# Hybrid decoder block: when the last gate/up products ask for the down projection's operands

## The chip, the cores and the metric

The kernel runs on one core of one Trainium2 chip. The metric is device microseconds (us) of one execution, lower is better. The kernel before took 987.95 us, the median of three runs (984.64, 988.54 and 987.95). Its profile is of a further execution, which took 985.37 us.

## The reference, cut to what matters

A sequence of 1024 tokens (after 16 meta tokens) of width 1024 goes through one decoder block in float32: a normalised mixer with two convolution groups, a residual, and then a SwiGLU feed-forward of width 2816 whose output is normalised, scaled by a gain and added to the residual. The change touches the feed-forward alone:

```python
def swiglu(xn, w_gate, w_up, w_down):
    a = jnp.einsum("btd,df->btf", xn, w_gate)
    u = jnp.einsum("btd,df->btf", xn, w_up)
    return jnp.einsum("btf,fd->btd", jax.nn.silu(a) * u, w_down)

        ff = swiglu(rms_norm(h, pre_ffn_norm[l]), w_gate[l], w_up[l], w_down[l])
        h = h + rms_norm(ff, post_ffn_norm[l])
```

## The kernel before, in words

**Arithmetic.** Each float32 operand is split into a rounded part (hi, written by ScalarE as a cast) and a rest (lo, written by VectorE as a difference), and one product of 128 by 128 by 512 is three matmuls: hi·hi, hi·lo, lo·hi (`mm3`, lines 106 to 110). The order of work on each engine is written out by hand: instructions stand on an engine in the order in which the Python code emits them, and each waits by semaphore for what it reads and for the buffer that it overwrites. A buffer belongs to a pool and a tag with a fixed number of copies, taken in turn.

**Gate and up.** The 2816 columns are 22 tiles of 128 (f tiles), taken as `NP` = 11 pairs; pair `j` holds f tiles `j` and `j + 11`. For each pair, gate and up are computed for two halves of the tokens and two halves of the 1024 inner columns by seven block products instead of eight. They are named 1, 6, 2, 5, 7, 3, 4 and run in this order from the third pair on; each is 24 matmuls, twelve for gate and twelve for up. After each product its sums leave PSUM (`Pair.leave`). With product 4 of a pair the SwiGLU outputs are complete, and `Pair.sums` forms the four sums S1 to S4 that the down projection needs of them, on GpSimd. `Pair.split` later turns each of the pair's seven results (A11, A12, A22, S1 to S4) into hi and lo and writes them to DRAM (`gdA`, `gdS`), hi through the buffer `HI`, which has four places.

**Down.** The down projection is seven block products too, in the order 1, 5, 2, 6, 7, 3, 4, each over 11 steps, one for each pair `j`. A step is 12 matmuls on four token tiles of 128. It reads `a`, 512 KB loaded back from DRAM by GpSimd's queue (`load`), and `db`, hi and lo of a sum of `w_down` tiles `wb`, which ScalarE and VectorE make two steps ahead (`side`, `LEAD` = 2). `a` goes into the tags `ws` and `wh` by turns, three copies each; `db` goes into the tag `wl`, three copies. In product 4, the last, the six last `j` of each token tile are kept for the end and run token tile by token tile, so that the epilogue of one tile runs beside the next; the `a` of `j` = 9 and 10 are put into `wl` there.

**Around the change from one to the other.** In the loop over pairs and products, `s` counts the products. With the last pair, `load_b` asks for `w_down`: 256 KB pieces on SyncE's queue for the first block of columns (`wb00`, `wb01`, `wb02`), 1 MB transfers on ScalarE's queue for later blocks (`wb10`, `wb11`). `gB_out` is the output gain, 512 KB, spread over 128 partitions. In `run`, at step `s` = 1, `last()` takes product 4 of the last pair out of PSUM, the ScalarE table is changed, and `gB_out` is multiplied by a constant on ScalarE (line 1124). The built program gives the transfers of SyncE and ScalarE eight completion semaphores in turn; the issue of one waits until the transfer that had its semaphore before has landed.

The lines that the steps below touch: 108 to 110 (matmuls), 644, 647, 650 (the add, subtract and multiply helpers), 767 and 769 (`glu`), 777 to 780 (`split`), 970 (`load_b`), 983 (`load`), 1024 and 1124 (`gB_out`), 1052 (output), 1099 and 1100 (`side`).

Of the kernel before, what the change touches and what calls it, by code (L numbers as in the profile page):

```python
# [9 lines left out]
F32R = mybir.dt.float32r  # L10
# [45 lines left out]
def hybrid_block(ctx: ExitStack, tc: tile.TileContext, xT, x, w_in, w_out, w_gate, w_up, w_down, par, g_post, g_ffn, g_out, out):  # L56
# [586 lines left out]
    def add(o, a, b, eng=None):  # L643
        (eng or nc.vector).tensor_tensor(o, a, b, op=ALU.add)  # L644
# [4 lines left out]
    def mul(o, a, b, eng=None):  # L649
        (eng or nc.vector).tensor_tensor(o, a, b, op=ALU.mult)  # L650
# [21 lines left out]
    class Pair:  # L672
# [62 lines left out]
        def leave(self, n, m, p):  # L735
            v, j = self.v, self.j
            if n == 1:
                v["U2", m] = piece(f"U2{j}{m}") if j % 2 else se.tile([P, 512], F32, tag="s", name=f"U2{j}{m}")
                nc.scalar.copy(v["U2", m], p)
            elif n == 6:  # L740
                add(v["U2", m], p, v["U2", m])
            elif n == 2:
                if m == 0:
                    v["G11"] = piece(f"G11{j}")
                    nc.scalar.activation(v["G11"], p, AF.Silu)
                else:
                    mul(v["G11"], p, v["G11"])
            elif n == 5:
                v["U4", m] = piece(f"U4{j}{m}")
                add(v["U4", m], p, v["U2", m])  # L750
            elif n == 7:
                v["C22", m] = piece(f"C22{j}{m}")
                add(v["C22", m], p, v["U4", m])
                self.glu("C22", m)
            elif n == 3:
                add(v["U4", m], p, v["U4", m])
                self.glu("U4", m)
            else:
                add(v["U2", m], p, v["U2", m])
                self.glu("U2", m)  # L760
                if m == 1:
                    self.sums()

        def glu(self, c, m):
            v = self.v
            if m == 0:
                nc.scalar.activation(v[c, 0], v[c, 0], AF.Silu)  # L767
            else:
                mul(v[c, 0], v[c, 0], v[c, 1], nc.gpsimd)

        def split(self, *names):

# [6 lines left out]
                nc.sync.dma_start(o[:, 0, :].bitcast(F32), hi.bitcast(F32))  # L779
                nc.sync.dma_start(o[:, 1, :].bitcast(F32), t)  # L780

        def sums(self):

            v = self.v

            v["A11"], v["A12"], v["S3"], v["A22"] = v["G11"], v["U2", 0], v["U4", 0], v["C22", 0]
            v["S1"] = piece(f"GS1{self.j}")
            add(v["S1"], v["S3"], v["A22"], nc.gpsimd)
            sub(v["S3"], v["A11"], v["S3"], nc.gpsimd)
            v["S2"] = piece(f"GS2{self.j}")  # L790
            sub(v["S2"], v["S1"], v["A11"], nc.gpsimd)
            v["S4"] = piece(f"GS4{self.j}")
            sub(v["S4"], v["A12"], v["S2"], nc.gpsimd)
            for k in [k for k in v if k not in names]:
                del v[k]

# [162 lines left out]

    HI, T4 = [], []  # L960
    WB = {}

    def load_b(b, g):

# [12 lines left out]
    later_splits = {6: ("A22", "S3", "S1"), 2: ("A11", "S2"), 5: ("A12",), 7: ("S4",)}  # L977
    loads = {}

    def load(n, an, j, tag):  # L980
        if (n, j) not in loads:
            loads[n, j] = wp.tile([P, 2, 512], F32R, tag=tag, name=f"a{n}_{j}")
            nc.gpsimd.dma_start(loads[n, j], gd[an][j])  # L983

    for s, (j, n) in enumerate(order):
        if s < 2:
            continue
        done = pairs[j].product(n, made.pop(s))
        if s == 2:
            results.pop(1)()  # L990
            turns(6, 7, at=(2, 7))()
            sums[4] = [pairs[0].a_side(6, m) for m in range(2)]
        if s == 14:
            pairs[first_splits[s][0]].split(*first_splits[s][1:])
        if s == len(order) - 1:
            for q in range(3):
                load(1, "A11", q, "ws")
        results.pop(s - 1, lambda: None)()
        if s == 15:
            pairs[first_splits[s][0]].split(*first_splits[s][1:])  # L1000
        if s == 2:
            for f in (t1_sum, t2_sum, t2_hi):
                for i in range(2, 4):
                    f(i)
            a_side(4)
            for i in range(2, 4):
                t2_lo(i)
        for f in extra.get(s, ()):
            f()
        a_side(s + LEAD)  # L1010
        if s in first_splits and s not in (14, 15):
            pairs[first_splits[s][0]].split(*first_splits[s][1:])
        elif j > 2:
            pairs[j - 1].split(*later_splits.get(n, ()))
        if j == NP - 1:
            for b, g in {2: ((0, 0), (0, 1)), 5: ((0, 2),), 3: ((1, 0),), 4: ((1, 1),)}.get(n, ()):
                load_b(b, g)
        results[s] = last = done

    rest = {3: "A11", 7: "S1", 14: "A12", 18: "S2", 25: "S3", 27: "S4", 29: "A22"}  # L1020


    gO = row(tp, "t", "gB_out", TT)[:, :D]
    nc.scalar.dma_start(gO, g_out.broadcast_to([P, D]))
    g0, g1 = gO[:, :512], gO[:, 512:]
    hold = {}

# [44 lines left out]
    def load_step(s):  # L1072
        if s < len(work):
            n, j, an = work[s][:3]
            load(n, an, j, "wl" if n == 4 and j >= 9 else ("ws", "wh")[s // 3 % 2])

    ready = {}

# [26 lines left out]
    def run():  # L1105
        bsum(0)
        for s in range(LEAD):
            sides(s)
        todo = []
        for s, (n, j_, _, _, mms) in enumerate(work):  # L1110
            for bank_, i, j, b, e, again, leave in mms:
                c = slice(i * P, (i + 1) * P)
                oa, ob = loads[n, j], made[n, j]
                mm3(bank_, oa[:, 0, c], oa[:, 1, c], ob[:, 0, :], ob[:, 1, :], b, e, again)
                if e and leave:
                    todo.append(lambda f=leave, i=i, b=bank_: f(i, b))
            load_step(s + AHEAD)
            if s in later_b:
                load_b(*later_b[s])
                use_b(*later_b[s])  # L1120
            if s == 1:
                last()
                table(AF.Abs_reciprocal_sqrt)
                nc.scalar.mul(gO, gO, RSCALE)
            sides(s + LEAD)
            if s in rest:
                pairs[NP - 1].split(rest[s])
            if n == 3:
                if j_ == 0:
                    for ti in range(4):  # L1130
                        residual(ti)
                sub(wd[j_][2], wd[j_][2], wd[j_][0])
                if j_ in (5, 6, 8, 9):
                    k = j_ if j_ < 7 else j_ - 1
                    side(4, k, wd[k][2])
            if mms and not mms[-1][4]:
                k = 1 if n == 4 and j_ > 1 else 2
                for g in [f() for f in todo[:k]]:
                    if g:
                        g()  # L1140
                todo = todo[k:]
                if after and not todo:
                    todo = after[:]
                    after.clear()
        finish4(todo)
        order_.close()
# [149 lines left out]
```

## Time and profile before

| what | number |
|---|---|
| three runs | 984.64, 988.54, 987.95 us |
| the profiled execution | 985.37 us, of which 983.6 us from its first to its last instruction (the span) |
| granted TensorE clock | 0.998 |
| TensorE busy | 964.9 us, 98% of the span |
| VectorE, ScalarE, GpSimd busy | 723.8, 397.9 and 280.5 us |
| moved by DMA | 156.68 MB, 159 GB/s in the mean |
| products of the last pair | up to 762 us into the span |
| down projection | 762 to 976 us |
| epilogue of the last token tile | 976 to 983.6 us |

Times in the timeline are microseconds from the start of the span. A matmul of 128 by 512 shows 0.39 us, but matmuls are pipelined: one starts every 0.227 us, so a step of twelve takes 2.72 us. Idle time of TensorE stands in square brackets at the matmul that ended it, with what released it. Time to landing is from the issue of a transfer until its completion semaphore.

### The profile page before, as it was taken

To read this page: it belongs to the slowest core of one execution; us is meant where nothing else is said; L and a number is where in the kernel's file an instruction comes from. 1 tells how busy PE (TensorE), PEld (TensorE's weight loads), DVE (VectorE), ACT (ScalarE), POOL (GpSimd) and SP (SyncE) were. 2 spreads that over 40 slices of the span, in tenths; PEclk is the share of its full clock that TensorE was granted. 3 is DMA by queue.
4 is the path that set the end of the run, shared out by engine and by line. 5 is a ranking of instruction groups with operands and counts; after the bars stand their busy time and mean duration, and the time that the engine had idled before them with its cause. 6 is when DMAs were issued, how large, how long until landed. Compare 5 with 4: busy or idle time off the path is not lost. (4 is left out here: it accounts for less than half of the span.)

```text
span 983.6 us, 12612 instructions
## 1 busy us (share of the span) xinstructions
PE 964.9 (98%) x4631; PEld 827.4 (84%) x4631; DVE 723.8 (74%) x1007; ACT 397.9 (40%) x657; POOL 280.5 (29%) x239
## 2 busy tenths in 40 slices
PE   9999999999999999989999999999999999999996
PEld 8999999998888878878888888888888788888884
DVE  6499999656464899999897887887886343546675
ACT  7433523254554663345343433433433333322331
POOL 0177964552000000443133132231242411111110
PEclk9999999999999999999999999999999999999999
DMA  8011111113442520446623623524319899856776
GB/s 305 22 43 45 45 48 59 65 43 123 156 163 85 179 89 0 171 172 224 223 109 129 224 107 141 187 112 172 151 46 338 276 357 368 261 174 211 278 226 244
DMA packets 59149, 156.68 MB, mean 159 GB/s; under 512 B 6224, under 2 KB 7504, under 8 KB 59088
## 3 DMA queue, kind: packets, MB, share of 16 engines
q1 hardware_dynamic: 42480, 104.02, 29.3%
q0 software_dynamic: 11088, 40.38, 12.7%
q10 hardware_dynamic: 5520, 11.48, 3.3%
q8 instruction: 36, 0.59, 0.2%
q14 instruction: 25, 0.20, 0.1%
HBM read 107.10 MB, written 48.76 MB: 158 GB/s over the span
## 5 line engine op out<-in xcount | busy, mean ns | idle before, releaser
L647 DVE TENSOR_TENSOR op<-u,op 128x512 fp32r<-128x512 f32 x154 | 145.2, 974 | 24.9 <-ACT op L660 23.9
L660 ACT CAST op<-u 128x512 fp32r<-128x512 f32 x154 | 91.9, 619 | 137.1 <-DVE u L647 79.6
L647 DVE TENSOR_TENSOR db<-wb,db 128x512 fp32r<-128x512 f32 x77 | 53.9, 705 | 93.4 <-ACT db L1099 93.1
L650 POOL TENSOR_TENSOR C<-C,C 128x512 f32<-128x512 f32 x11 | 17.6, 1596 | 319.6 <-ACT C L767 172.8
L1099 ACT CAST db<-wb 128x512 fp32r<-128x512 f32 x77 | 47.1, 620 | 120.0 <-PE qx L110 55.7
L108 PE MATMUL qx<-db,a 128*128 128x512 f32 x176 | 68.7, 390 | 3.6 <-DMA a<-gdA 2.3
L109 PE MATMUL qx<-db,a 128*128 128x512 f32 x176 | 68.6, 390 | 0.2 <-DVE db L647 0.2
L110 PE MATMUL qx<-db,a 128*128 128x512 f32 x176 | 68.5, 389 | 0.0
L644 DVE TENSOR_TENSOR U<-y,U 128x512 f32<-128x512 f32 x66 | 43.6, 683 | 20.8 <-PE y L110 20.8
L650 POOL TENSOR_TENSOR U<-U,U 128x512 f32<-128x512 f32 x22 | 31.6, 1435 | 89.3 <-ACT U L767 60.1
L109 PE MATMUL qy<-db,a 128*128 128x512 f32 x132 | 51.4, 389 | 0.0
L110 PE MATMUL qy<-db,a 128*128 128x512 f32 x132 | 51.4, 389 | 0.0
L108 PE MATMUL qy<-db,a 128*128 128x512 f32 x132 | 51.4, 389 | 0.0
L983 POOL DMA_DIRECT2D a<-gdS x44 | 23.3, 529 | 91.2 <-PE qy L110 45.9
L108 PEld LDWEIGHTS qx<-db,a 128*128 128x128 f32 x176 | 33.0, 188 | 11.1 <-issue 2.7
L372 DVE SCALAR_TENSOR_TENSOR ac<-g,pr,ac 128x512 f32<-128x512 f32 x56 | 42.1, 752 | 0.0
L372 DVE SCALAR_TENSOR_TENSOR ae<-d,pr,ae 128x512 f32<-128x512 f32 x56 | 42.1, 751 | 0.0
L647 DVE TENSOR_TENSOR u<-u,u 128x512 f32<-128x512 f32 x44 | 39.0, 907 | 0.8
L109 PEld LDWEIGHTS qx<-db,a 128*128 128x128 f32 x176 | 33.0, 188 | 7.4 <-DVE db L647 0.5
L110 PEld LDWEIGHTS qx<-db,a 128*128 128x128 f32 x176 | 33.0, 188 | 6.8
L109 PE MATMUL y<-T2l,op 128*128 128x512 f32 x88 | 34.4, 391 | 1.8 <-DVE T2l L647 1.8
L110 PE MATMUL y<-T1h,op 128*128 128x512 f32 x88 | 34.4, 390 | 1.6 <-DVE op L647 1.6
(309 smaller groups left out, 2928.5 us busy)
## 6 DMA issues: line engine op xcount, KB each, us to landing
a<-gdS POOLq DMA_DIRECT2D x44, 512.0 KB, 3.9
a<-gdA POOLq DMA_DIRECT2D x33, 512.0 KB, 6.8
u<-w_gate_u SPq DMA_DIRECT2D x22, 512.0 KB, 5.2
u<-w_up_u SPq DMA_DIRECT2D x22, 512.0 KB, 6.1
gdS<-HI SPq DMA_DIRECT2D x44, 256.0 KB, 2.4
gdA<-HI SPq DMA_DIRECT2D x33, 256.0 KB, 2.0
gdS<-GS SPq DMA_DIRECT2D x33, 256.0 KB, 2.5
ws_o<-w_out_u SPq DMA_DIRECT2D x14, 512.0 KB, 4.9
```

The lines of the kernel that those rows point to most:

```text
L108: nc.tensor.matmul(o, lh, rh, start=start, stop=False, skip_group_check=again)
L109: nc.tensor.matmul(o, lh, rl, start=False, stop=False, skip_group_check=again)
L110: nc.tensor.matmul(o, ll, rh, start=False, stop=stop, skip_group_check=again)
L372: nc.vector.scalar_tensor_tensor(out if i == n - 1 else acc, src[:, i : i + HALF], w(i), init if i == first else acc, op0=ALU.mult, op1=AL ...
L644: (eng or nc.vector).tensor_tensor(o, a, b, op=ALU.add)
L647: (eng or nc.vector).tensor_tensor(o, a, b, op=ALU.subtract)
L650: (eng or nc.vector).tensor_tensor(o, a, b, op=ALU.mult)
L660: nc.scalar.copy(t[:, 0, :], src)
L983: nc.gpsimd.dma_start(loads[n, j], gd[an][j])
L1099: nc.scalar.copy(t[:, 0, :], b)
```

## The change

1. The loads of `a` for the first four steps: `j` = 0 and 1 are asked for with product 7 of the last pair, not product 4, and `j` = 3 with product 4, not after it.
2. `w_down`: `wb00` and `wb01` with product 6, not 2; `wb02` with 2, not 5; `wb10` with 5, not 3; `wb11` with 7, not 4.
3. `gB_out` is asked for with product 2 of the last pair, not after the loop.
4. In `run`, `sides(s + LEAD)` stands ahead of `last()` and the table change at `s` = 1, so that `db` of step 3 is made first.
5. The last pair's final multiply and its four sums move from GpSimd to VectorE; the sums stand at `s` = 2.
6. The `a` of `j` = 9 and 10 of down product 4 go into a tile of their own in the pool `xg` (no copy more than before: a place whose `w_down` tile is done with), asked for at step 3 of product 3.

```diff
@@ -758,15 +758,15 @@
-                if m == 1:
-                    self.sums()
+                if m == 1 and j < NP - 1:
+                    self.sums(nc.gpsimd)
 
         def glu(self, c, m):
             v = self.v
             if m == 0:
                 nc.scalar.activation(v[c, 0], v[c, 0], AF.Silu)
             else:
-                mul(v[c, 0], v[c, 0], v[c, 1], nc.gpsimd)
+                mul(v[c, 0], v[c, 0], v[c, 1], None if (self.j, c) == (NP - 1, "U2") else nc.gpsimd)
@@ -779,18 +779,18 @@
-        def sums(self):
+        def sums(self, eng=None):
 
             v = self.v
 
             v["A11"], v["A12"], v["S3"], v["A22"] = v["G11"], v["U2", 0], v["U4", 0], v["C22", 0]
             v["S1"] = piece(f"GS1{self.j}")
-            add(v["S1"], v["S3"], v["A22"], nc.gpsimd)
-            sub(v["S3"], v["A11"], v["S3"], nc.gpsimd)
+            add(v["S1"], v["S3"], v["A22"], eng)
+            sub(v["S3"], v["A11"], v["S3"], eng)
             v["S2"] = piece(f"GS2{self.j}")
-            sub(v["S2"], v["S1"], v["A11"], nc.gpsimd)
+            sub(v["S2"], v["S1"], v["A11"], eng)
             v["S4"] = piece(f"GS4{self.j}")
-            sub(v["S4"], v["A12"], v["S2"], nc.gpsimd)
+            sub(v["S4"], v["A12"], v["S2"], eng)
@@ -977,9 +978,17 @@
     def load(n, an, j, tag):
         if (n, j) not in loads:
-            loads[n, j] = wp.tile([P, 2, 512], F32R, tag=tag, name=f"a{n}_{j}")
+            if n == 4 and j >= NP - 2:
+                if not late_a:
+                    late_a.append(blocks(big("a4")))
+                k = 2 * (j - NP + 2)
+                loads[n, j] = late_a[0][:, k : k + 2, :]
+            else:
+                loads[n, j] = wp.tile([P, 2, 512], F32R, tag=tag, name=f"a{n}_{j}")
             nc.gpsimd.dma_start(loads[n, j], gd[an][j])
@@ -993,8 +1002,8 @@
         if s == len(order) - 1:
-            for q in range(3):
-                load(1, "A11", q, "ws")
+            load(1, "A11", 2, "ws")
+            load(1, "A11", 3, "wh")
         results.pop(s - 1, lambda: None)()
@@ -1005,6 +1014,9 @@
+        if s == len(order) - 3:
+            for q in range(2):
+                load(1, "A11", q, "ws")
@@ -1012,16 +1024,18 @@
+        if (j, n) == (NP - 1, 2):
+            last_gain.append(row(tp, "t", "gB_out", TT)[:, :D])
+            nc.scalar.dma_start(last_gain[0], g_out.broadcast_to([P, D]))
         if j == NP - 1:
-            for b, g in {2: ((0, 0), (0, 1)), 5: ((0, 2),), 3: ((1, 0),), 4: ((1, 1),)}.get(n, ()):
+            for b, g in {6: ((0, 0), (0, 1)), 2: ((0, 2),), 5: ((1, 0),), 7: ((1, 1),)}.get(n, ()):
                 load_b(b, g)
@@ -1072,7 +1086,7 @@
-            load(n, an, j, "wl" if n == 4 and j >= 9 else ("ws", "wh")[s // 3 % 2])
+            load(n, an, j, ("ws", "wh")[s // 3 % 2])
@@ -1118,17 +1132,22 @@
+            sides(s + LEAD)
             if s == 1:
                 last()
                 table(AF.Abs_reciprocal_sqrt)
                 nc.scalar.mul(gO, gO, RSCALE)
-            sides(s + LEAD)
+            if s == 2:
+                pairs[NP - 1].sums()
             if s in rest:
                 pairs[NP - 1].split(rest[s])
             if n == 3:
                 if j_ == 0:
                     for ti in range(4):
                         residual(ti)
+                if j_ == 3:
+                    for j in range(NP - 2, NP):
+                        load(4, "A22", j, None)
```

**ScalarE, from the last pair into the down projection.** `op` casts are operands of the last pair's products, `HI` casts belong to the splits of pair 9, `db_0` to `db_5` are the hi parts for steps 0 to 5 of down product 1, and the row without operands changes the function table. Before:

```order
L970 DMA wb_6431<-w_down_u 128x4x512
L1024 DMA gB_out<-g_out 128x1024
L1099 CAST db_0_6449<-wb_6268 128x512
L1099 CAST db_1_6452<-wb_6268 128x512
L1099 CAST db_2_6469<-wb_6268 128x512
L767 ACTIVATE U_6204<-U_6204 128x512
L117 ACT_TABLE_LOAD
L117 ACTIVATE pr<-pr 128x1
L1124 ACTIVATE gB_out<-gB_out 128x1024
L1099 CAST db_3_6499<-wb_6268 128x512
L1099 CAST db_4_6516<-wb_6273 128x512
```

With the change, from the `HI` cast ahead of `wb10` on (`gB_out` was asked for five rows sooner):

```order
L971 DMA wb_6325<-w_down_u 128x4x512
L660 CAST op_100_6361<-u_5797 128x512
L660 CAST op_101_6363<-u_5799 128x512
L777 CAST HI<-GS_6170 128x512
L971 DMA wb_6371<-w_down_u 128x4x512
L767 ACTIVATE C_6399<-C_6399 128x512
L767 ACTIVATE U_6353<-U_6353 128x512
L1113 CAST db_0_6449<-wb_6226 128x512
L1113 CAST db_1_6452<-wb_6226 128x512
L1113 CAST db_2_6469<-wb_6226 128x512
L1113 CAST db_3_6486<-wb_6226 128x512
L767 ACTIVATE U_6204<-U_6204 128x512
```

The cast of `db_3` has moved ahead of the last Silu, the table change and the scaling of `gB_out`; the two 1 MB requests now stand ahead of and between the casts of the last pair's operands and splits.

**VectorE, steps 1 and 2 of the down projection.** Before, the lo parts of `db_3` to `db_5` (line 647) followed the two adds of `last()` at once, and the multiply and the sums (`GS` and `U` rows) were GpSimd's. With the change:

```order
L647 TENSOR_TENSOR db_3_6486<-wb_6226,db_3_6486 128x512
L644 TENSOR_TENSOR U_6204<-x_6327,U_6204 128x512
L644 TENSOR_TENSOR U_6206<-x_6340,U_6206 128x512
L650 TENSOR_TENSOR U_6204<-U_6204,U_6206 128x512
L647 TENSOR_TENSOR db_4_6509<-wb_6231,db_4_6509 128x512
L644 TENSOR_TENSOR GS_6512<-U_6353,C_6399 128x512
L647 TENSOR_TENSOR U_6353<-G_6310,U_6353 128x512
L647 TENSOR_TENSOR GS_6515<-GS_6512,G_6310 128x512
L647 TENSOR_TENSOR GS_6517<-U_6204,GS_6515 128x512
L647 TENSOR_TENSOR db_5_6535<-wb_6231,db_5_6535 128x512
L647 TENSOR_TENSOR G_6310<-G_6310,HI 128x512
```

Between the lo parts of `db_3` and `db_5` VectorE now has five instructions more, four of them ahead of `db_5`.

**GpSimd, the end of the down projection.** `gdA` here are the A22 pieces of product 4. Before, the last requests of the queue:

```order
L983 DMA a_7_7832<-gdA_7_2310 128x1024
L983 DMA a_8_7852<-gdA_8_2311 128x1024
L983 DMA a_9_7860<-gdA_9_2312 128x1024
L983 DMA a_10_7862<-gdA_10_2313 128x1024
L1292 UNCONDITIONAL_BRANCH
```

With the change, in the middle of product 3's requests (`gdS` 7 to 9 are product 3's):

```order
L992 DMA a_7_7600<-gdS_7_2354 128x1024
L992 DMA a_7605<-gdA_9_2312 128x1024
L992 DMA a_7605<-gdA_10_2313 128x1024
L992 DMA a_8_7621<-gdS_8_2355 128x1024
L992 DMA a_9_7639<-gdS_9_2356 128x1024
```

The two requests now stand twelve requests sooner, and `a_8` of product 4 is the queue's last.

More of the change, by code (lines that the diff above doesn't have):

```diff
@@ L961, in hybrid_block @@
     WB = {}
+    last_gain = []
     def load_b(b, g):
@@ L978, in hybrid_block @@
     loads = {}
+    late_a = []
     def load(n, an, j, tag):
         if (n, j) not in loads:
-            loads[n, j] = wp.tile([P, 2, 512], F32R, tag=tag, name=f"a{n}_{j}")
+            if n == 4 and j >= NP - 2:
[5 more added lines that the diff above has]
+                loads[n, j] = wp.tile([P, 2, 512], F32R, tag=tag, name=f"a{n}_{j}")
             nc.gpsimd.dma_start(loads[n, j], gd[an][j])
@@ L1020, in hybrid_block @@
     rest = {3: "A11", 7: "S1", 14: "A12", 18: "S2", 25: "S3", 27: "S4", 29: "A22"}
-    gO = row(tp, "t", "gB_out", TT)[:, :D]
-    nc.scalar.dma_start(gO, g_out.broadcast_to([P, D]))
+    gO = last_gain[0]
     g0, g1 = gO[:, :512], gO[:, 512:]
```

## The prediction

> **What bounds the kernel now.** I read the totals by engine, then TensorE's waits, then the timelines around the two waits at lines that the change touches.
>
> ```profile
> PE 964.9 (98%) x4631; PEld 827.4 (84%) x4631; DVE 723.8 (74%) x1007; ACT 397.9 (40%) x657; POOL 280.5 (29%) x239
> PE qx L108 <- DMA a<-gdA: 2.3, 1, 2.3
> PE y L109 <- DVE T2l L647: 1.8, 1, 1.8
> ...
> PE qx L108 <- ACT db L1099: 1.3, 1, 1.3
> ...
> PE qx L109 <- DVE db L647: 0.2, 1, 0.2
> ```
>
> TensorE is busy for 98% of the span, so an edit that takes no matmul away is worth only TensorE's waits. Only the three `qx` rows lie in the down projection, 2.3, 1.3 and 0.2 us; `T2l` is at the start of gate and up. This caps the gain near 4 us, plus what matmuls lose while they resume. The first wait, on TensorE, ScalarE and ScalarE's queue:
>
> ```profile
> 770.07 0.39 PE L110 MATMUL qx<-db,a 128*128 128x512 f32 x1
> 771.74 0.50 PE L108 MATMUL qx<-db,a 128*128 128x512 f32 x1 [1.28 <-ACT db L1099]
> 772.46 0.50 PE L109 MATMUL qx<-db,a 128*128 128x512 f32 x1 [0.22 <-DVE db L647]
> ...
> 773.03 0.39 PE L108 MATMUL qx<-db,a 128*128 128x512 f32 x1
> ...
> 764.36 0.63 ACT L767 ACTIVATE U<-U 128x512 f32<-128x512 f32 x1 [1.36 <-DVE U L644]
> 765.01 1.28 ACT L117 ACT_TABLE_LOAD   x1
> 770.12 1.06 ACT L1124 ACTIVATE gB_out<-gB_out 128x1024 f32<-128x1024 f32 x1 [3.61 <-DMA gB_out<-g_out]
> 771.08 1.64 ACT L1099 CAST db<-wb 128x512 fp32r<-128x512 f32 x3
> ...
> gB_out<-g_out ACTq DMA_DIRECT2D x1, 512.0 KB, 14.8
> ```
>
> ScalarE stands in order. It waits 3.61 us for `gB_out`, which took 14.8 us to land, scales it, and only then makes `db_3`, which TensorE wanted at 770.30. The second wait, with the chain that ended last and GpSimd's queue:
>
> ```profile
> 957.31 0.39 PE L108 MATMUL qx<-db,a 128*128 128x512 f32 x1
> 960.49 0.39 PE L110 MATMUL qx<-db,a 128*128 128x512 f32 x1
> 963.17 0.47 PE L108 MATMUL qx<-db,a 128*128 128x512 f32 x1 [2.30 <-DMA a<-gdA]
> 975.99 0.39 PE L110 MATMUL qx<-db,a 128*128 128x512 f32 x1
> ...
> 952.33 1.05 POOL L983 DMA_DIRECT2D a<-gdA  x2 [2.19 <-PE qx L110]
> 955.05 0.53 POOL L983 DMA_DIRECT2D a<-gdA  x1 [1.67 <-PE qx L110]
> ...
> 955.05 7.99 DMA a<-gdA
> ```
>
> The first token tile of the closing part starts `j` = 5 at 957.31 and needs `a_10` at 960.72. `a_10` could be asked for only when `wl` came free, at 955.05, and landed 7.99 us later.
>
> **The change, part by part.** The pace: between the matmuls of 764.63 (below) and 770.07 lie two steps, 24 matmuls in 5.44 us: one every 0.2267, a step in 2.72.
>
> *`db_3` ahead of the table and the gain (edits 3 and 4).* Without the wait, the fourth matmul of step 3 starts at 770.30 + 3 × 0.2267 = 770.98, not 773.03. Worth **2.05 us**, if `db_3` is early. In step 0 and in a later step:
>
> ```profile
> 764.63 0.39 PE L110 MATMUL qx<-db,a 128*128 128x512 f32 x1
> ...
> 774.85 0.39 PE L110 MATMUL qx<-db,a 128*128 128x512 f32 x1
> 775.27 0.62 ACT L1099 CAST db<-wb 128x512 fp32r<-128x512 f32 x1 [2.03 <-PE qx L110]
> 775.93 0.69 DVE L647 TENSOR_TENSOR db<-wb,db 128x512 fp32r<-128x512 f32 x1 [1.71 <-ACT db L1099]
> ```
>
> A cast that waits for its `wl` place starts 0.42 us after the last matmul of the step that frees it, and the difference 0.66 later. `db_3` takes the place of `db_0`, so it runs from 764.63 + 0.42 = 765.05 and is whole at 766.4, 4 us early. Next on ScalarE: VectorE's adds of `last()` start at 766.3 behind it, not 763.64, the Silu at 767.0, table 1.28, the small activation, and the gain from 769.2 (it has landed long before); then `db_4` from 770.2, wanted at 773.02. So the gain of edit 3 covers `db_4`: its ready time must be under 771.4.
>
> *Multiply and sums on VectorE (edit 5).* Removed: five GpSimd operations, the first and last of which are
>
> ```profile
> 765.08 1.28 POOL L650 TENSOR_TENSOR U<-U,U 128x512 f32<-128x512 f32 x1 [4.14 <-ACT U L767]
> 770.29 1.27 POOL L647 TENSOR_TENSOR GS<-U,GS 128x512 f32<-128x512 f32 x1
> 771.50 1.66 POOL L983 DMA_DIRECT2D a<-gdA  x3
> ...
> L647 DVE TENSOR_TENSOR wb<-wb,wb 128x512 f32<-128x512 f32 x44 | 30.1, 685 | 0.0
> ...
> 689.10 1.74 POOL L644 TENSOR_TENSOR GS<-U,C 128x512 f32<-128x512 f32 x1
> 689.61 1.77 DVE L647 TENSOR_TENSOR op<-u,op 128x512 fp32r<-128x512 f32 x1
> ```
>
> The loads behind them go out when their place is free (from 765.05), not at 771.5; no TensorE wait there, so 0. On VectorE one costs 0.685 us, 0.60 from start to start. The multiply (767.7) fits before `db_4` (770.8 to 771.5); four sums reach 773.9; `db_5` is then whole near 774.6. TensorE wants its lo part at 773.02 + 2.72 + 0.23 = 775.97. Cost **0**, with 1.3 us of cover. Beyond the row: an operation beside a GpSimd one took 1.77, and four at that price would end 4.3 later and stall 3.0 us. GpSimd has no arithmetic left there, so I take 0.685; bounds 0 and +3.0.
>
> *`a_9` and `a_10` of product 4 (edit 6).* First matmul with `a_10`: 960.72 instead of 963.17. From there 57 matmuls remain, so the last would start at 960.72 + 56 × 0.2267 = 973.41, not 975.99. Worth **2.58 us**, if nothing else is late. Next late is `a_8`: asked for at 952.33, wanted at 957.31 + 9 × 0.2267 = 959.35, 7.0 later; it made that with `a_9` and `a_10` in flight behind it and has 1 MB less beside it. The two loads now stand ahead of a load of product 3, some 40 us before their use, wait for VectorE's last read of a `w_down` tile of product 7, which lies before product 3, and put 1 MB into a stretch (860 to 945) which moved 212 GB/s; the last row is of all loads of `a`:
>
> ```profile
> 919.69 0.53 POOL L983 DMA_DIRECT2D a<-gdS  x1 [2.19 <-PE qy L110]
> ...
> DMA packets 4946, 18.01 MB, mean 212 GB/s; under 512 B 559, under 2 KB 559, under 8 KB 4942
> ...
> DMA to landing us min/median/max: 3.5/4.9/10.0
> ```
>
> A load is asked for when the place used six steps before comes free, five steps (13.6 us) ahead; at 10.0 it still has 3.6. Cost 0; bound, two loads' median more (9.8) and the wait 6.2. I take 0, since 1 MB at the 380 GB/s of the fullest stretch (below) is 2.8 us.
>
> The Trainium skill, DMA: Bandwidth & Descriptors, "Anatomy of one DMA", fits a load of this queue as 2.0 us + bytes / 436,000 per us: 3.2 us for 512 KB as an estimate. By it alone `a_10` would land at 958.3, in time, and edit 6 be worth 0 wherever nothing shares the engines (sum 2.05). The trace's 7.99 differs and decides; what it leaves of this is in the first rival.
>
> *Earlier transfers (edits 1 and 2).* They remove no wait. They fill an emptier stretch before one that is full:
>
> ```profile
> 756.40:770.30 13.90, 13.90 (x63) 11.30 (x61) 4.88 (x6) 3.71 (x7) 8.28 (x9) 1.00 1.04 380
> ...
> 741.83 3.78 SPq L970 DMA_DIRECT2D wb<-w_down_u  x8
> SPq L779 <- DMA wb<-w_down_u: 3.0, 2, 2.8
> ...
> wb<-w_down_u SPq DMA_DIRECT2D x11, 256.0 KB, 5.6
> ...
> 743.94 0.62 ACT L660 CAST op<-u 128x512 fp32r<-128x512 f32 x1
> 746.02 0.62 ACT L660 CAST op<-u 128x512 fp32r<-128x512 f32 x1 [1.46 <-PE y L110]
> ```
>
> SyncE's eight requests now go out some 5 us sooner than 741.83, one every 0.47, ahead of a split's stores, and the ninth request in turn waits for the first to land (the 3.0 us row). Behind them: the stores, and through `HI`'s four places the next casts into it. On ScalarE, `wb10` waits for a piece of `wb01` asked for near 740, ahead of the operand cast of 743.94. At the 5.6 us median of a piece that is 745.6, and cast and difference make the operand by 747.0. TensorE wants it when the last product starts: step 0 starts at 764.63 − 11 × 0.2267 = 762.14, and 24 matmuls sooner is 756.70. Cost 0, with 9.7 us of cover. In GpSimd's queue the load of `a_3` now stands ahead of a multiply; its place is an operand of product 7, done with when product 3 starts, at 751.26, before the request. Also 0.53 us for `gB_out`'s request ahead of a Silu, under the same cover.
>
> **Sum.** 2.05 + 2.58 = 4.63 us. The span becomes 983.6 − 4.6 = 979.0, and the profiled execution 985.4 − 4.6 = 980.7. The median is 987.95, 2.6 above it: if the excess is the same afterwards, 983.3; if it is made of the same late transfers, 980.7. I see no row for it and take the middle, **982.0 us**, 0.6% under the median.
>
> **Rivals.**
> - *One transfer was hidden anyway, or its successor is late* (`a_8`, or `db_4` behind the gain): one term stays away. For: `a` landed in 3.5 to 10.0 us, so 7.99 is no fixed price, and `a_8`'s 7.0 is narrow. Against: less in flight. 983.3 to 985.9 from the two bases, 984.4. Chance 0.17.
> - *VectorE's queue*: the sums push `db_5` past 775.97, with the same on the steps behind. It decides when each of four costs over 0.33 us more than 0.60. Up to +3.0 of the 4.6: 982 to 985. Chance 0.08.
> - *Slower: ScalarE held at two requests.* Place: `wb10` waits for a piece of `wb01`, and `wb11` for a store that now queues behind all eight pieces; ScalarE, in order, reaches two Silus and `db_0` only after both. Those and the difference take some 2.4 us and TensorE wants `db_0` at 762.14, so it decides from a second hold that ends after 759.7, and the whole gain is gone at 764.4. For: `gB_out` took 14.8 us in the full stretch, and all these transfers now fall together. If each hold lasts as long as that, from 740 to 769.6, TensorE waits 9.9 us: less 4.6 it is 5.3 slower, 990.7 on the profile's base and 993.2 on the median's. Against: before 756 there was room, and pieces land in 5.6. Chance 0.07.
>
> **How the numbers follow.** Forecast 0.68, its own range 979.8 to 984.0; the rivals 0.17, 0.08 and 0.07. The range, 979.5 to 986.0, takes in the first two rivals and leaves out the slow one. A measurement of this kernel tells about 0.5% from no change, that is 983.0 and 992.9. Of the forecast some 0.46 lies below 983.0 and 0.22 above; of the first two rivals 0.04 below and 0.21 above; of the slow one 0.05 above 992.9 and 0.02 below. Faster 0.50, same 0.45, slower 0.05.
>
> **What would show it.** In the waits of TensorE both large `qx` rows are gone; step 3 starts 2.72 after step 2; the closing part runs 72 matmuls without a bracket; `gB_out` is scaled with no wait for DMA; and VectorE's four sums end before 774.5. Wrong would be a bracket of TensorE on `op` or `db` between 740 and 780, or one on `a` in product 3 or at `a_8`, or a span over 981.

## The result, and the profile after

The changed kernel takes 980.54 us (median of seven executions, 979.97 to 981.41), the kernel before 988.54 us beside it (seven, 984.64 to 993.52). The ratio is 0.992, with a 95% interval of 0.9898 to 0.9941: 0.8% faster. The profiled execution takes 980.54 us with a span of 978.8, where 980.7 and 979.0 were forecast as the sum of the two terms; the predicted time, 982.0, is 1.5 us high.

Totals, and TensorE's waits (releaser, then us in total, times, longest), in the changed kernel:

```profile
PE 964.4 (99%) x4631; PEld 827.6 (85%) x4631; DVE 726.8 (74%) x1012; ACT 398.1 (41%) x657; POOL 274.2 (28%) x234
...
PE y L110 <- DVE op L647: 1.6, 1, 1.6
PE warm L88 <- POOL xh L229: 1.4, 1, 1.4
PE y L109 <- DVE T2l L647: 1.0, 1, 1.0
PE x L108 <- ACT U L739: 1.0, 1, 1.0
PE po L108 <- DVE cv L433: 0.7, 1, 0.7
PE p_g L108 <- ACT xh L183: 0.6, 1, 0.6
PE p_v L108 <- ACT wh_v L210: 0.5, 1, 0.5
PE p_c L110 <- POOL wl_c L154: 0.3, 1, 0.3
```

This is the whole list of waits: all `qx` rows are gone. What is left, 1.6 us and less each, lies ahead of the down projection and, but for the 0.5 us of `p_v`, stood there before. The timeline of the first wait's place:

```profile
769.89 0.39 PE L110 MATMUL qx<-db,a 128*128 128x512 f32 x1
770.11 0.39 PE L108 MATMUL qx<-db,a 128*128 128x512 f32 x1
...
764.87 0.62 ACT L1113 CAST db<-wb 128x512 fp32r<-128x512 f32 x1 [2.05 <-PE qx L110]
...
768.91 1.04 ACT L1139 ACTIVATE gB_out<-gB_out 128x1024 f32<-128x1024 f32 x1
769.86 1.13 ACT L1113 CAST db<-wb 128x512 fp32r<-128x512 f32 x2
...
773.15 0.69 DVE L647 TENSOR_TENSOR GS<-U,GS 128x512 f32<-128x512 f32 x1
773.76 0.69 DVE L647 TENSOR_TENSOR db<-wb,db 128x512 fp32r<-128x512 f32 x1
```

`db_3` is cast at 764.87, its step begins at 770.11 without a bracket, the gain is scaled with no wait for DMA (it landed 7.1 us after its request), and the fourth sum ends at 773.84. One thing went otherwise than the prediction worked it out. SyncE, ScalarE and VectorE around `wb10`:

```profile
737.75 7.61 SPq L971 DMA_DIRECT2D wb<-w_down_u  x8
...
750.85 0.39 ACTq L971 DMA_DIRECT2D wb<-w_down_u  x1
751.28 1.14 ACT L660 CAST op<-u 128x512 fp32r<-128x512 f32 x2 [5.48 <-PE x L110]
...
751.93 1.30 DVE L647 TENSOR_TENSOR op<-u,op 128x512 fp32r<-128x512 f32 x2 [4.13 <-ACT op L660]
```

The eight pieces took 7.61 us to ask for, not 3.78. ScalarE stood from 745.8 to 750.85 at the request of `wb10` (the bracket names TensorE, which had long been done). The trace shows what freed it: the piece that had the same completion semaphore before was asked for at 743.89 and landed at 750.83. So the operand that was to be whole by 747.0 was whole at 753.2. TensorE wanted it 24 matmuls ahead of the down projection's first, at 761.95 − 5.44 = 756.5. Of 9.7 us of cover 3.3 were left.

So the sum came out, but the median fell by 8.0 us, not by 4.6. The experiments had two questions: which edits carry the gain, and where the other 3.4 us come from.

### The profile page after: what moved, and what is told of

Its sections match the earlier page's. It is cut to its first block, busy times and chain, and to the rows that moved or that the text cites. A ratio compares the mean times of both kernels' runs of the same rounds, so it can differ in the third digit from the quotient of the medians.

```text
span 978.8 us, 12605 instructions
## 1 busy us (share of the span) xinstructions
PE 964.4 (99%) x4631; PEld 827.6 (85%) x4631; DVE 726.8 (74%) x1012; ACT 398.1 (41%) x657; POOL 274.2 (28%) x234
## 4 chain that ended last, share of the span: by engine, by line
PE 81%; DVE 12%; issue 2%; ACT 2%; DMA 2%; POOL 1%; SPq 0%; ACTq 0%; DVEq 0%; POOLq 0%
PE x L110 6%; PE x L108 6%; PE x L109 6%; PE y L110 6%; PE y L109 6%; PE y L108 6%; PE qx L109 4%; PE qx L108 4%; PE qx L110 4%; PE qy L109 3%; PE qy L108 3%; PE qy L110 3%; PE po L108 2%; PE po L109 2%; PE po L110 2%; DVE ac L372 2%
## 5 line engine op out<-in xcount | busy, mean ns | idle before, releaser
L108 PE MATMUL x<-B21h,op 128*128 128x512 f32 x88 | 34.4, 391 | 1.0 <-ACT U L739 1.0
```

The lines of the kernel that those rows point to most:

```text
L108: nc.tensor.matmul(o, lh, rh, start=start, stop=False, skip_group_check=again)
```

## Experiments

### The kernel before, once more

> The kernel before once more, for a second profiled execution. Its runs lie between 984.6 and 993.5 us, those with the change between 980.0 and 981.4. Theory (what the prediction's working leaves open): what a run of the kernel before has above 980.5 is the two waits alone, which vary with the time to landing of two transfers. Then this profile shows TensorE's waits at the same two rows in the down projection (for db behind the gain, and for a of the last product), larger together by what its time is larger than 985.4, and the other waits as before, within 0.3 us. Rival: some further wait, in the down projection's first steps or at the start of the program, carries the rest; then a row of TensorE's waits appears that the first profile lacks.

988.84 us (twelve executions, 986.3 to 993.3), ratio 0.9999 (0.9981 to 1.0017). Its profiled execution, of 987.9 us, differs from the first one. TensorE's waits, its timeline and its granted clock (the last three columns of a window are PEclk, DMA share and GB/s):

```profile
PE qx L108 <- ACT db L1099: 3.3, 1, 3.3
...
PE qx L108 <- DMA a<-gdA: 1.2, 1, 1.2
```

```profile
769.27 0.39 PE L110 MATMUL qx<-db,a 128*128 128x512 f32 x1
772.93 0.80 PE L108 MATMUL qx<-db,a 128*128 128x512 f32 x1 [3.28 <-ACT db L1099]
...
774.25 0.63 PE L110 MATMUL qx<-db,a 128*128 128x512 f32 x1
774.67 0.63 PE L108 MATMUL qx<-db,a 128*128 128x512 f32 x1
...
778.94 0.40 PE L109 MATMUL qx<-db,a 128*128 128x512 f32 x1
```

```profile
772.00:776.00 4.00, 3.07 (x7) 2.17 (x8) 2.50 (x4) 2.44 (x5) 0.35 (x1) 0.52 1.07 332
```

`gB_out` landed after 16.8 us instead of 14.8, so the first wait is 3.28 us instead of 1.28. After it matmuls follow each other every 0.427 us instead of 0.227, for some 5 us, at a granted clock of 0.52. The matmul of 778.94 is the fourteenth after that of 769.27; at the usual pace it would have started at 769.27 + 14 × 0.2267 = 772.44. The wait of 3.28 us cost 6.5, and the one for `a_10`, here 1.16 us, cost 1.4: together 7.9 us, where the span is 7.3 us above the changed kernel's. No further wait appears, so the rival falls; but the two waits are longer by only 0.6 us together where the execution is 2.5 us longer, so the theory fails too as it stood: what a wait costs is not its length.

The Trainium skill, TensorE: Matmul & The Clock Gate, "What's actually happening", says that TensorE's clock falls to one half after at least one idle window of about 3.4 us and comes back after a busy one. The half rate agrees with 0.427 against 0.227; the length of the idle time does not, as the next run shows.

In these twelve executions the span goes from 984.5 us with a mean granted clock of 0.997 to 991.5 with 0.991. In the seven of the changed kernel it stays between 978.2 and 979.6, with 0.998 and 0.999. The spread of the kernel before, and its median's excess over the first profiled execution, go with the clock. The slowest execution of this kernel that was profiled took 987.9 us; what those above it waited for was not seen.

### Edit 6 alone, edit 4 alone, and the two together

```diff
@@ edit 6 alone (before +)
-            load(n, an, j, "wl" if n == 4 and j >= 9 else ("ws", "wh")[s // 3 % 2])
+            load(n, an, j, ("ws", "wh")[s // 3 % 2])
...
+                if j_ == 3:
+                    for j in range(NP - 2, NP):
+                        load(4, "A22", j, None)
@@ edit 4 alone (before +)
+            sides(s + LEAD)
             if s == 1:
                 last()
                 table(AF.Abs_reciprocal_sqrt)
                 nc.scalar.mul(gO, gO, RSCALE)
-            sides(s + LEAD)
```

> Edit 6 alone on the kernel before: the a of j = 9 and 10 of the last product in a tile of their own, asked for in product 3. Prediction's term: 2.6 us, so a profile with a span of 981.0 in which the wait for a is gone and the one for db (1.3 + 0.2) stays. If the spread of the kernel before comes from this load, the timed runs draw together to about 983 (within 2 us) and the median gains 5 to 6; if it comes from the gain's transfer, they stay spread over 5 us or more with a median near 986.

> Edit 4 alone: db of step 3 ahead of the table change and the gain; the gain's transfer stays where it was, and so stands in front of db of step 4. Prediction's working: db of step 3 is early, the gain lands near 770.1 and its scaling ends near 771.2, so that db of step 4 is cast by 771.9 and TensorE, which wants it at 773.0, does not wait: gain 2.05 us, span near 981.6. Rival: the gain lands later than that in some executions (it did 14.8 us after its request in the one profiled), the wait moves to step 4, and edit 4 alone gains less than 2 us; the timed runs stay spread.

> Edits 4 and 6 alone, without the earlier transfers (1, 2, 3) and with the sums on GpSimd. Prediction: edits 1, 2 and 5 are worth 0, so this has the whole gain: span 979.0, timed median 980.5 to 981, a spread under 2 us. Rival: the earlier transfers carry part of the gain; then this stays 2 us or more above the changed kernel, with a wait for a, for db or behind the gain left in the first steps of the down projection.

**Edit 6 alone**: 984.97 us (983.47 to 987.59), ratio 0.995 (0.9934 to 0.9967). The wait for `a_10` is gone, the first wait stands:

```profile
772.31 0.50 PE L108 MATMUL qx<-db,a 128*128 128x512 f32 x1 [2.42 <-ACT db L1106]
773.03 0.50 PE L109 MATMUL qx<-db,a 128*128 128x512 f32 x1 [0.23 <-DVE db L647]
...
774.30 0.62 PE L108 MATMUL qx<-db,a 128*128 128x512 f32 x1
...
777.70 0.40 PE L110 MATMUL qx<-db,a 128*128 128x512 f32 x1
```

The pace falls here too, only 2.0 us after TensorE has resumed, and for 3.4 us. The 2.65 us of wait cost 4.85 by the count of matmuls. In the first profiled execution 2.30 us of wait cost 2.58: the edge lies between. The spread, 4.1 us, is neither of the two that were expected (2 us, or 5 and more): both transfers fed it.

**Edit 4 alone**: 984.87 us (983.52 to 989.77), ratio 0.9964 (0.9945 to 0.9982). **4 and 6**: 982.24 us (981.2 to 983.54), ratio 0.993 (0.991 to 0.9951). With `db_3` ahead of it, the gain holds up `db_4`. In the kernel with edit 4 alone `gB_out` lands after 16.8 us and is scaled late:

```profile
771.35 1.06 ACT L1125 ACTIVATE gB_out<-gB_out 128x1024 f32<-128x1024 f32 x1 [2.97 <-DMA gB_out<-g_out]
...
772.32 1.12 ACT L1099 CAST db<-wb 128x512 fp32r<-128x512 f32 x2
```

TensorE waits 1.18 us for `db_4` in that kernel and 1.21 in the one with both. And the last Silu now stands behind `db_3`, so GpSimd's multiply and sums run later, and the loads behind them. GpSimd's and TensorE's timeline with both:

```profile
773.60 2.19 POOL L990 DMA_DIRECT2D a<-gdA  x4
...
789.97 0.47 PE L108 MATMUL qx<-db,a 128*128 128x512 f32 x1 [1.35 <-DMA a<-gdA]
```

Four loads go out at 773.60 (771.50 before), and a wait for `a` appears at 789.97 that the kernel before does not have. Moving the cast alone trades one wait for two smaller ones.

### Edits 3 and 6 alone

```diff
@@ before +
+        if (j, n) == (NP - 1, 2):
+            last_gain.append(row(tp, "t", "gB_out", TT)[:, :D])
+            nc.scalar.dma_start(last_gain[0], g_out.broadcast_to([P, D]))
...
-    gO = row(tp, "t", "gB_out", TT)[:, :D]
-    nc.scalar.dma_start(gO, g_out.broadcast_to([P, D]))
+    gO = last_gain[0]
...
+                if j_ == 3:
+                    for j in range(NP - 2, NP):
+                        load(4, "A22", j, None)
```

> Kernel before plus edits 3 and 6. Theory (the first wait is one late gain: ScalarE stands in order, so an early gB_out is as good as db_3 put ahead of it): gB_out has landed before the table, the gain is scaled by about 767.6, db_3 is made by 768.5 against 770.3 wanted, TensorE waits at none of db_3, db_4, a_10; span 979 to 979.5, median 980.5 to 981, as the whole change. Rival (the late loads of a behind GpSimd's sums bite, as they did beside edit 4): a wait of 0.6 to 1.4 us for a near 789, span 980 to 981, median 981.5 to 982.5.

980.27 us (979.67 to 980.83), ratio 0.9899 (0.9858 to 0.9939), span 979.1: as fast as the whole change. ScalarE:

```profile
765.11 1.28 ACT L117 ACT_TABLE_LOAD   x1
...
766.51 1.04 ACT L1134 ACTIVATE gB_out<-gB_out 128x1024 f32<-128x1024 f32 x1
767.47 0.60 ACT L1109 CAST db<-wb 128x512 fp32r<-128x512 f32 x1
```

Asked for at 738.70, the gain lands in 4.2 us. Behind it `db_3` is made 2 us ahead of its use, in the old order. GpSimd's four loads go out at 772.45, and no step waits for them.

### One edit undone in the changed kernel

```diff
@@ edit 5 undone
-                if m == 1 and j < NP - 1:
+                if m == 1:
                     self.sums(nc.gpsimd)
...
-                mul(v[c, 0], v[c, 0], v[c, 1], None if (self.j, c) == (NP - 1, "U2") else nc.gpsimd)
+                mul(v[c, 0], v[c, 0], v[c, 1], nc.gpsimd)
...
-            if s == 2:
-                pairs[NP - 1].sums()
@@ edit 2 undone
-            for b, g in {6: ((0, 0), (0, 1)), 2: ((0, 2),), 5: ((1, 0),), 7: ((1, 1),)}.get(n, ()):
+            for b, g in {2: ((0, 0), (0, 1)), 5: ((0, 2),), 3: ((1, 0),), 4: ((1, 1),)}.get(n, ()):
@@ edit 3 undone
-            last_gain.append(row(tp, "t", "gB_out", TT)[:, :D])
-            nc.scalar.dma_start(last_gain[0], g_out.broadcast_to([P, D]))
...
+    gO = row(tp, "t", "gB_out", TT)[:, :D]
+    nc.scalar.dma_start(gO, g_out.broadcast_to([P, D]))
```

> Changed kernel with edit 5 undone: the last pair's multiply and sums on GpSimd again. Theory (edit 5 is not worth 0: the loads of a queue behind the sums, as beside edit 4 alone): GpSimd's sums end near 773.5, the loads behind them go out there, TensorE waits 0.6 to 1.4 us for a near 789; span 979.5 to 980.5, median 981 to 982. Rival (the prediction's 0: with gB_out and w_down sooner the stretch is emptier and the late loads land in time): no wait for a, span 978.8 to 979.2, median 980.5.

> Changed kernel with edit 2 undone: the tiles of w_down asked for at products 2, 5, 3, 4 again. Theory (edit 2 worth 0): ScalarE is no longer held for 5 us at wb10's request near 745, the loads of 756 to 770 are fuller, db_3 to db_5 are in time all the same; span 978.8 to 979.3. Rival (edit 2 carries part of the gain: wb of db_3 to db_5 or the loads of a land late): one or two waits of 0.5 to 1.5 us for db or a between 765 and 795, span 979.5 to 981.

> Changed kernel with edit 3 undone: gB_out asked for where the kernel before asks. Theory (the gain stands ahead of db_4 on ScalarE): gB_out lands near 770 to 771.5, is scaled by 771 to 772.5, db_4 is late and TensorE waits 0.3 to 1.2 us for it near 773; span 979.3 to 980.3, median 981 to 982. Rival (with w_down sooner the queue is free and gB_out lands by 767): no wait, span 978.8 to 979.2.

**Edit 5 undone**: 981.12 us (980.32 to 981.59), ratio 0.9908 (0.9874 to 0.9942). One wait comes back, sooner than expected, and put down to ScalarE's cast of 777.21, which is for a later step:

```profile
777.93 0.47 PE L108 MATMUL qx<-db,a 128*128 128x512 f32 x1 [0.77 <-ACT db L1113]
...
773.56 2.19 POOL L992 DMA_DIRECT2D a<-gdA  x4
```

The trace shows that it is the late load: the first of the four, the `a` of this step, was asked for at 773.56 and landed 4.24 us later, at 777.80, and TensorE went on 0.13 us after that, as it did after `a_10` in the first profile (963.04 and 963.17). The wait is 0.77, the cost in this execution 1.06 by the count of matmuls.

**Edit 2 undone**: 979.8 us (979.5 to 979.99), ratio 0.9895 (0.9862 to 0.9929), span 978.2. No `qx` wait. ScalarE is held at `wb10` here too, until 753.14, 0.02 us after the transfer that had its semaphore before has landed, but it holds up nothing: the operand casts of product 3 stand ahead of it, at 741.46, 743.17 and 745.25, and the Silu behind it waits for VectorE's add until 754.1. Edit 2 is worth nothing beside the others.

**Edit 3 undone**: 980.14 us (979.7 to 980.33), ratio 0.9899 (0.9865 to 0.9932). The expected wait for `db_4` did not come:

```profile
768.70 1.04 ACT L1137 ACTIVATE gB_out<-gB_out 128x1024 f32<-128x1024 f32 x1
...
769.65 1.13 ACT L1111 CAST db<-wb 128x512 fp32r<-128x512 f32 x2
```

`gB_out` was asked for at 754.5 and landed 14.1 us later, at 768.6, just as ScalarE came to it.

### Edits 3 and 4 both undone

```diff
@@ changed kernel, edit 3 undone as above, and
-            sides(s + LEAD)
             if s == 1:
                 last()
                 table(AF.Abs_reciprocal_sqrt)
                 nc.scalar.mul(gO, gO, RSCALE)
+            sides(s + LEAD)
```

> Changed kernel with edits 3 and 4 both undone (1, 2, 5 and 6 left). Theory (either of the two is enough, one is needed): gB_out is asked for at about 754.5 and lands 14 to 17 us later, db_3 stands behind the gain and TensorE waits 0.5 to 3 us for it near 770 to 773; span 979.5 to 983, median 981 to 984. Rival (edit 2 empties the queue ahead of it, so the earlier w_down alone removes the wait): no wait for db, span 978.6 to 979.

981.57 us (981.12 to 982.27), ratio 0.9913 (0.9886 to 0.9941). The first wait is back, but small:

```profile
768.41 1.06 ACT L1136 ACTIVATE gB_out<-gB_out 128x1024 f32<-128x1024 f32 x1 [2.69 <-DMA gB_out<-g_out]
...
770.02 0.50 PE L108 MATMUL qx<-db,a 128*128 128x512 f32 x1 [0.37 <-ACT db L1111]
770.75 0.50 PE L109 MATMUL qx<-db,a 128*128 128x512 f32 x1 [0.23 <-DVE db L647]
```

`gB_out` landed in 14.3 us. In the two kernels with edits 1, 2 and 5 and without edit 3 it took 14.1 and 14.3; in five profiles of kernels without any of these 14.8, 15.9, 16.5, 16.8 and 16.8. So edits 1, 2 and 5 together take most of the first wait away, which the prediction had at nothing. That it is the earlier `w_down` is not shown: edit 1 takes two of six 512 KB loads of `a` out of the same stretch, and no run that asks for `gB_out` late has the one without the other. This group, edit 3 and edit 4 all work on one wait: with 2 or 3 undone alone the others cover it, and with 3 left alone of them, in the kernel of edits 3 and 6, it is covered too.

### Edit 6 undone

```diff
@@ changed kernel
-            load(n, an, j, ("ws", "wh")[s // 3 % 2])
+            load(n, an, j, "wl" if n == 4 and j >= 9 else ("ws", "wh")[s // 3 % 2])
...
-                if j_ == 3:
-                    for j in range(NP - 2, NP):
-                        load(4, "A22", j, None)
```

> Changed kernel with edit 6 undone: a_9 and a_10 of product 4 in the four places of wl again. Theory (an independent wait, priced once): TensorE waits 1.2 to 2.5 us for a_10 near 958 to 960; if under 2.4 it costs itself plus 0.3, span 980.3 to 981.5; median 981.5 to 983, and a wider spread from run to run than the changed kernel's 1.4 us, since a wait over 2.4 costs 2 more. Rival (the wait was that of the loads piled up behind product 4 in the kernel before only): none, span 978.8.

986.81 us (ten executions, 985.67 to 987.6), ratio 0.9967 (0.9949 to 0.9985): 6.3 us slower than the changed kernel by the medians, more than either theory gave, and with a spread of 1.9 us, not the wider one that was expected. (The kernel before had a median of 989.7 us beside it, and 988.5 beside the changed kernel; by the two ratios the difference is 4.6 us.) TensorE, and the load in the chain of waits:

```profile
957.39 0.39 PE L110 MATMUL qx<-db,a 128*128 128x512 f32 x1
961.99 0.76 PE L108 MATMUL qx<-db,a 128*128 128x512 f32 x1 [4.21 <-DMA a<-gdA]
...
967.95 0.40 PE L110 MATMUL qx<-db,a 128*128 128x512 f32 x1
```

```profile
951.95 9.90 DMA a<-gdA
```

In four profiled executions `a_10` took 6.84, 7.58, 7.99 and 9.90 us to land, and TensorE waited 1.16, 1.89, 2.30 and 4.21: always the landing less 5.68 or 5.69, as the prediction's 960.72 − 955.05 = 5.67 has it. The 4.21 us are over the edge. The matmul of 967.95 is the fifteenth after 957.39, at the usual pace due at 960.79, so the wait cost 7.2. That is what the profiled span has above the changed kernel's, 985.1 against 978.8, within 0.9 us. Why the load is slowest in this kernel, whose ten spans all lie at 983.9 to 985.8, is open; no run tells it.

### `w_down` sooner still

```diff
@@ changed kernel
-            for b, g in {6: ((0, 0), (0, 1)), 2: ((0, 2),), 5: ((1, 0),), 7: ((1, 1),)}.get(n, ()):
+            for b, g in {6: ((0, 0), (0, 1)), 2: ((0, 2), (1, 0)), 5: ((1, 1),)}.get(n, ()):
```

> Changed kernel with the last three w_down requests a product or more sooner: wb10 together with wb02 at product 2, wb11 at product 5. Tests the slower rival's hold: ScalarE, in order, stands at wb10's request until a piece of wb01 lands, now ahead of the Silu of G and the operand casts of product 3. Theory (the hold only eats cover: 3.3 us was left of 9.7 in the changed kernel): the hold begins some 2 to 4 us sooner and is as long or longer, ends by about 751, and TensorE waits under 0.5 us for op; span 978.5 to 979.5. Rival (the hold is the price of early requests): ScalarE held past 753 and TensorE stops 1 to 5 us on op or db between 745 and 765; span 980 to 985.

984.22 us (982.11 to 985.5), ratio 0.9937 (0.9915 to 0.9959): 3.7 us slower than the changed kernel by the medians, 1.7 by the two ratios; the spans, 980.3 to 983.7, lie all above the changed kernel's. ScalarE and TensorE:

```profile
750.03 0.39 ACTq L971 DMA_DIRECT2D wb<-w_down_u  x1
750.52 0.60 ACT L745 ACTIVATE G<-x 128x512 f32<-128x512 f32 x1 [11.20 <-DMA gdA<-HI]
752.48 1.28 ACT L660 CAST op<-u 128x512 fp32r<-128x512 f32 x2 [1.36 <-DVE u L647]
...
753.15 0.79 PE L108 MATMUL y<-B22h,op 128*128 128x512 f32 x1 [2.52 <-ACT op L660]
753.74 0.63 PE L109 MATMUL y<-B22l,op 128*128 128x512 f32 x1
```

The request leaves ScalarE at 750.03, almost when it does in the changed kernel (750.85), and again 0.02 us after the landing of an earlier piece that had its semaphore, asked for at 742.88. But now the Silu of G stands behind it as well and ScalarE idles 11.2 us, so the whole chain of product 3 is late. TensorE waits 2.52 us and goes on at 0.427, and loses 4.3 by the count of matmuls. So the hold of the prediction's slower rival is real, and with one request two products sooner it costs time.

### Waits put in on purpose

```diff
@@ changed kernel
+    dose = {27: 16, 38: 18, 49: 19, 61: 21}
...
+            if s in dose:
+                jd = piece(f"jd{s}")
+                for _ in range(dose[s]):
+                    nc.scalar.mul(jd, g0, 1.0)
             sides(s + LEAD)
```

> Changed kernel with idle work on ScalarE (16, 18, 19 and 21 extra 512-wide activations of the gain, results unused) ahead of one operand cast each in products 2, 6, 7 and 3 of the down projection, where transfers are light; output unchanged. At about 0.52 us each, TensorE then waits some 1.6, 2.7, 3.2 and 4.2 us for db. Theory (a wait beyond some 2.4 us halves TensorE's granted clock afterwards, wherever it stands): after the first wait matmuls stay 0.227 us apart and the wait costs itself plus at most 0.6; after each of the other three they stand 0.427 apart for some 3 us and each costs 2 to 3 us more than its wait; span about 997 to 1000. Rival (the slow pace came with the full transfers of 756 to 780, not with the length of the wait): 0.227 after all four, span 978.8 + 11.7 + about 1 = 991 to 992.

One execution, 1013.84 us, span 1012.1. An activation took 0.66 us, not 0.52, so the waits are longer than planned, and none is short:

```profile
844.58 0.50 PE L108 MATMUL qx<-db,a 128*128 128x512 f32 x1 [3.56 <-ACT db L1114]
...
881.85 0.79 PE L108 MATMUL qy<-db,a 128*128 128x512 f32 x1 [4.93 <-ACT db L1114]
...
883.16 0.63 PE L110 MATMUL qy<-db,a 128*128 128x512 f32 x1
883.59 0.63 PE L108 MATMUL qy<-db,a 128*128 128x512 f32 x1
```

```profile
881.00:885.00 4.00, 3.15 (x7) 2.23 (x8) 3.18 (x6) 1.93 (x4) 0.00 (x0) 0.50 0.00 0
```

After all four (3.79, 4.93, 5.58 and 8.83 us) matmuls stand 0.427 apart, in this window at a clock of 0.50 with no DMA at all; the DMA share is 0.01 or less behind the last two as well. They cost 5.97, 7.77, 8.05 and 11.47, in all 33.3 us, and 978.8 + 33.3 is the span, 1012.1. The rival, that the full transfers slow TensorE, falls. The lower end of the edge was not tried by this run.

## Why the prediction was right, and where not

- **The two terms on the path** were right for the execution that they were read from: 978.8 against 979.0, each wait removed. That the sum came out to 0.2 us is in part luck: a wait at the start of gate and up, which no edit touches, was 1.8 us in the one profile and 1.0 in the other. As prices they were too small, and so was the cap "near 4 us". "Worth 2.58 us" for edit 6 is 6.3 when it alone is undone (986.81 − 980.54); "Worth 2.05 us" for edits 3 and 4 is 1.0 with edits 1, 2 and 5 left in (981.57 − 980.54), 4.4 when edits 1 to 5 are all undone (984.97 − 980.54). The terms do not add, since the landing that each wait hangs on differs from execution to execution, and a wait over the edge costs 1.8 to 3.3 us more than itself. The medians compared here were not taken side by side; what holds without them is the count of matmuls: each profiled span, less what its waits in the table below cost, is 977.5 to 979.1 us, in all fourteen profiles, the changed kernel's (978.8) among them.
- **The median's excess** was the step that failed: "I see no row for it and take the middle". The changed kernel's median equals its profiled execution. The excess was made of the same late transfers, which the prediction gave as one of two ends (980.7 against 980.54 measured). What it did not have is the clock: each landing late enough for a wait beyond the edge costs 1.8 to 3.3 us on top. One profiled execution, by chance with waits of 1.50 and 2.30 us, showed none of this.
- **"Cost 0" for edits 1, 2 and 5** holds for edit 2 undone alone (979.8). Edit 5 undone brings a wait of 0.77 us and a median 0.6 higher, with the two ranges overlapping. But they were said to remove no wait, and the three together nearly remove the first one (0.60 us of wait left with edits 3 and 4 undone). Edit 1 was not tried apart; edits 3 and 6 alone do without it.
- **VectorE's queue**: sums done at 773.84 and `db_5` at 774.45, where 773.9 and 774.6 were worked out. Each sum took 0.68 or 0.69 us; no operation stood beside a GpSimd one.
- **The hold of ScalarE**: "by 747.0 ... with 9.7 us of cover" was wrong by 6.2 us. The median landing of a piece, 5.6 us, came from an emptier stretch than the one the edit makes (336 GB/s at a DMA share of 1.01 in 735 to 756, where it was 316 at 0.91), and SyncE's eight requests took twice as long. The conclusion held on what was left, 3.3 us. The slow rival's place was right, but its point, a second hold past 759.7, was not the first to decide: in the run with `w_down` sooner still the operands of product 3 were late first.
- **The successor** (`a_8`) was in time, as forecast, and no wait for `a` came in product 3. The 1 MB that edit 6 puts there shows: loads of product 3 took up to 9.2 us, where the kernel before had up to 8.3, both within the 13.6 us that they are asked for ahead.

The smallest set tried that gives the whole gain is edits 3 and 6 (980.27). The change without edit 2 has the lowest median, 979.8; its interval, 0.9862 to 0.9929, holds the changed kernel's 0.992, so it is not shown to be faster.

## What to carry to other kernels

Price a TensorE wait by its spread over executions, and by what follows it: here a wait of up to 2.30 us cost itself plus 0.6 at most, and one from 2.52 on cost 1.8 to 3.3 us more. Where one late transfer holds up an engine that works in order, asking for that transfer sooner was the simplest cure here; several cures for one wait cover each other, so undoing them one by one shows nothing until all are undone. A transfer asked for earlier on an engine that also computes can hold that engine at the request until an older transfer lands: count what is queued behind the request, not only the request.

## What the runs showed of the hardware

Waits of TensorE in the last pair and the down projection, and what they cost, by counting matmuls at 0.2267 us (two brackets one matmul apart are added):

| kernel | wait, us | cost, us | matmuls 0.427 apart after it |
|---|---|---|---|
| edits 3 and 4 undone | 0.60 | 1.16 | no |
| edit 4 alone | 0.65 | 0.92 | no |
| edit 5 undone | 0.77 | 1.06 | no |
| before, second profile | 1.16 | 1.43 | no |
| edit 4 alone | 1.18 | 1.77 | no |
| edits 4 and 6 | 1.21 | 1.77 | no |
| edits 4 and 6 | 1.35 | 1.65 | no |
| before, first profile | 1.50 | 2.06 | no |
| edit 4 alone | 1.89 | 2.15 | no |
| before, first profile | 2.30 | 2.58 | no |
| `w_down` sooner still | 2.52 | 4.29 | yes |
| edit 6 alone | 2.65 | 4.85 | yes |
| before, second profile | 3.28 | 6.53 | yes |
| put in | 3.79 | 5.97 | yes |
| edit 6 undone | 4.21 | 7.21 | yes |
| put in | 4.93 | 7.77 | yes |
| put in | 5.58 | 8.05 | yes |
| put in | 8.83 | 11.47 | yes |

The extra cost does not grow with the wait. From the first matmul after the wait to the return of the usual pace it takes 3.1 to 6.0 us, and the slow pace can set in late: 2.0 us after TensorE resumed with edit 6 alone, at once in most of the others. With 18 waits the edge between 2.30 and 2.52 us is that of these runs, not a constant shown; the 2.65 us of edit 6 alone are brackets of 2.42 and 0.23, so counted by the longest single one the edge lies between 2.30 and 2.42.

The same 512 KB transfer of `gB_out` landed in 4.2 to 8.0 us when asked for near 738 to 742, and in 14.1 to 16.8 near 754 to 755, behind 2 MB of `w_down` on the same queue. The stretch where it lands late (756.4 to 770.3) has a DMA share of 1.02 to 1.07 in those kernels, the one where it lands early (735 to 756) 0.87 to 1.03 in the others. So the fuller stretch alone hardly tells the two apart, and no run asks for it late with the queue free.
